# First value stage of an encoder trunk: the norm's vector on GpSimd's queue, the first products reordered, weights piece by piece for both token halves

## The chip, the core and the metric

The kernel runs on one core of a Trainium2 chip. The core has a matrix engine (TensorE, PE in the profile; PEld is its weight load), a vector engine (VectorE, DVE), a scalar engine (ScalarE, ACT), GpSimd (POOL) and SyncE (SP). Each takes its instructions in order from its own queue; SP, ACT and POOL can issue transfers, and all transfers run on the same 16 DMA engines. The metric is the device time of one execution in microseconds (us); lower is better. Times in the profile count from the start of the profiled span.

## The reference, cut to what matters

The input x is one sequence of 256 tokens by 1024 channels in float32. Two layers run, each with two sub-layers, then a last norm. What the change touches is the start of the first sub-layer: a norm and the value columns of one wide projection.

```python
def _rmsnorm(x, g):
    y = x * lax.rsqrt(jnp.mean(x * x, axis=-1, keepdims=True) + EPS)
    return y * g

for layer in range(DEPTH):                       # DEPTH = 2
    h = h + _token_mixer(_rmsnorm(h, norm1[layer]), w_in[layer], ...)
    h = h + _conv_ffn(_rmsnorm(h, norm2[layer]), ...)
return _rmsnorm(h, norm_f)

def _token_mixer(xn, w_in, ...):
    u, q, k, v, g_pool, g_attn = jnp.split(xn @ w_in, SPLITS, axis=-1)
    # pooling mixer on u; sliding-window attention on q, k, v in 3 groups of 4 heads
    # of 128; both branches gated by sigmoids and projected
    return merged @ w_o
```

The columns of v are 1536 wide: three groups of 512, one for each group of heads.

## The kernel before, in words

**Products.** Float32 accuracy is had from a pass format in which an operand is split into a rounded high part and the rest, the low part. A product of two such operands is three matrix multiplications: high by high ("hh"), low x by high weight ("lh"), high x by low weight ("hl"). ACT makes high parts, DVE makes low parts. Almost all of the kernel's work on PE is of this kind, 128 x 128 by 128 x 512.

**Tokens and channels.** The 256 tokens are two halves (t = 0 and 1) of 128, the 1024 channels eight chunks (k = 0 to 7) of 128. A value group is 2 halves x 8 chunks x 3 multiplications = 48 products, which add up in two tiles of PSUM; three groups make 144.

**The first stage** works on x before its norm is known: the gain vector of the norm is multiplied into the weights as they are split (lines 251 to 264), and the tokens' factor 1/rms is applied to the sums when they leave PSUM (`keep_values`, line 945). `begin` (line 367) issues the first transfers: the gain vector (8 rows of 128, tile `grows`) on ACT's queue, then x's first quarter of channels (256 wide) for t = 1 on ACT's queue and for t = 0 on SP's, then alternately first weights (`raw0`, in four chunks) and x (tile `h`), then `raw1` in two parts, `raw2`, `raw3`. PE meanwhile multiplies a constant (line 403, the warm-up), turns the gain vector into a column (line 394; DVE keeps it as `gcol`, line 395), and turns x chunk by chunk (line 787, tile `xt_ps`); ACT casts the turned x to its high part `xuh` (line 793), DVE makes its low part `xul` (line 794).

`begin_values_of_x` (line 767) is an order written out by hand for the first group: `split`, `both`, `turn_x`, `products` and `square` are called one by one, and every engine gets its instructions in that order. `both(k)` makes the high part of weight chunk k on ACT and its low part on DVE; chunk 0's high part is made on DVE (line 261). `square` takes the sum of squares of half a token's channels, on ACT for the first half and on DVE for the second (lines 804 and 808), and GpSimd makes 1/rms (`rs`, tile `rstd`) of them. `whole` adds `xuh` and `xul` to a float32 x (line 822). At the end the four pieces of the second group (two chunks each; `wh` and `wl` 4 to 7) are split.

`first_values` (line 900) turns 1/rms into rows (line 908, `r_ps`), scales x by it and the gain into `x2`, the normed x that the q, k and u projections use (lines 912 to 918), and multiplies groups two and three: for each group all four pieces are fetched, then all products of t = 0, then all of t = 1 (line 930). This function is outside the hand-written order: a scheduler places its instructions. `load_params` (line 409) follows: nine small transfers on SP's queue, and for each layer a turn on PE (line 418) and copies on DVE. `build_bias` (line 424) begins with four transfers and some fifty small copies on GpSimd.

**Weights.** The class `Weights` loads 1 MB at a time into three buffers (`raw`), splits into five pairs of buffers (`wh`, `wl`) and looks three pieces ahead, four where `by_hand` is set. Where `by_hand` is 0 its instructions are also tied behind others (`queue_behind`).

After the third group PE goes on with u, q and k (tile `t_ps`), in a hand-written order again.

Of the kernel before, what the change touches and what calls it, by code (L numbers as in the profile page):

```python
# [10 lines left out]
F32 = mybir.dt.float32  # L11
# [25 lines left out]
WARM = ((P,) * 6, (P // 2,), (P // 2,))  # L37
# [243 lines left out]
def encoder(ctx, tc, x, w_in, w_pool, pool_scale, w_a, w_b, w_o, norm1, norm2, w_up, conv_w,  # L281
# [85 lines left out]
    def begin():  # L367
# [8 lines left out]
        nc.scalar.dma_start(out=rows8, in_=norm1[0].rearrange("(k p) -> k p", p=P))  # L376
# [15 lines left out]
        ps = mmp.tile([P, P], F32, tag="mm", name="gain_ps")  # L392
        warm(ps, ones, WARM[0])
        nc.tensor.transpose(ps[:, 0:KD], rows8, ident[:KD, :KD])
        nc.vector.tensor_copy(gcol, ps[:, 0:KD])
        ps = mmp.tile([P, P], F32, tag="mm", name="warm_ps")
        warm(ps, ones, WARM[1])
        return lambda widths: warm(ps, ones, widths)
# [10 lines left out]
    def load_params():  # L409

        nc.sync.dma_start(out=edge.rearrange("p a b -> p (a b)"), in_=edges[0].partition_broadcast(P))
        for l in range(DEPTH):
# [3 lines left out]
            nc.sync.dma_start(out=rowst[88:96, :], in_=pool_scale[l].rearrange("(f p) -> f p", p=P))  # L416
            pt = mmp.tile([P, 512], F32, tag="mm", name="prm_ps")
            nc.tensor.transpose(pt[:, :96], rowst, ident[:96, :96])
            nc.vector.tensor_copy(prm[:, l, :], pt[:, :96])
            nc.vector.tensor_scalar_mul(hps[:, l, :], prm[:, l, 88:96], 0.5)  # L420

# [345 lines left out]
    def begin_values_of_x():  # L767


        more = begin()  # L770
# [29 lines left out]
        def square(t, n):  # L800
            cc = HALVES[n]
            junk = sm.tile([P, 512], F32, tag="p", bufs=3, name="junk")
            if n == 0:
                nc.scalar.activation(
                    junk, h[:, t, cc], AF.Square, scale=D**-0.5, accum_out=ss[t][:, n : n + 1]
                )
            else:
                nc.vector.scalar_tensor_tensor(
                    out=junk, in0=h[:, t, cc], scalar=1.0 / D, in1=h[:, t, cc],
                    op0=ALU.mult, op1=ALU.mult, accum_out=ss[t][:, n : n + 1],  # L810
                )
# [40 lines left out]

        every = ("hh", "lh", "hl")
        keep = [turn_x((t,), 0, 2) for t in range(2)]
        more(WARM[2])
# [44 lines left out]
    def first_values(rs, raw_x, fs, done, pe, keep_values):  # L900
# [19 lines left out]
        for g in range(NG):  # L920
            held = [W.get() for _ in range(4)] if g + 1 < NG else []
            for t in range(2):
                keep_values(t, g, ps[t], rs)
# [571 lines left out]
```

## Time and profile before

| what | us |
|---|---|
| median of 3 runs | 854.85 (854.73 to 855.8) |
| the profiled execution's own time | 854.77 |
| its span, first to last instruction | 853.0 |
| PE busy in the span | 844.8 |
| DVE, ACT, POOL busy | 620.6, 490.5, 33.6 |
| first product of the first group begins | 5.73 |
| u, q, k products begin | 41.31 |

In rows of the chain in order of time, the columns are start, length, and what ran or was waited for, with a count. In rows of the timeline they are start, length, engine, line, operation, tiles written and read, shapes and count; a bracket tells how long the engine had been idle before it and what ended that. Rows of windows give for a stretch its length, the busy time of PE, PEld, DVE, ACT and POOL with counts, PE's granted clock, the DMA engines' busy share and GB/s. An engine's name with q (SPq, ACTq) is its queue of transfers. PE's matmuls overlap: a product is listed with 0.39 us, but the next starts 0.227 us later.

### The profile page before, as it was taken

The page shows a single profiled execution, that of the slowest core. Times are in us where ns is not written, and L with a number is a line of the kernel's source. Part 1 is how long each engine was busy: PE and PEld are TensorE (multiplying, and loading weights), DVE is VectorE, ACT ScalarE, POOL GpSimd, SP SyncE. Part 2 cuts the span into 40 slices and gives each one's busy share as a digit, 9 for nine tenths or more (in the row PEclk, how much of TensorE's full clock was granted, in tenths as well). Part 3 has the DMA queues.
Part 4 walks back from the last instruction along what each step waited for, and adds up shares of the span by engine and source line. Part 5 has one row for each costly group of instructions (what it writes and reads, how often), then busy time and mean ns, then how long its engine had stood idle before and what let it go on. Part 6 is the DMA issues. An engine that isn't in the chain of part 4 may idle for free.

```text
span 853.0 us, 11006 instructions
## 1 busy us (share of the span) xinstructions
PE 844.8 (99%) x3925; PEld 705.7 (83%) x3925; DVE 620.6 (73%) x885; ACT 490.5 (58%) x723; POOL 33.6 (4%) x96
## 2 busy tenths in 40 slices
PE   9999999999999999999999999999999999999997
PEld 7888888888888888888888888888888888888885
DVE  7958777757765976878655687868567767777774
ACT  7744566654543865657545454577454556556663
POOL 1700000000010000000000000000000100000000
PEclk9999999999999999999999999999999999999999
DMA  9699997895657879986726899868777489799941
GB/s 326 212 302 285 294 292 233 252 293 210 222 209 263 300 250 301 293 284 233 245 100 216 261 280 330 245 226 264 242 257 269 147 289 315 230 288 288 296 145 50
DMA packets 147678, 214.03 MB, mean 251 GB/s; under 512 B 7768, under 2 KB 68640, under 8 KB 147624
## 3 DMA queue, kind: packets, MB, share of 16 engines
q1 hardware_dynamic: 147320, 212.93, 76.8%
q8 instruction: 31, 0.51, 0.2%
q10 hardware_dynamic: 304, 0.40, 0.1%
q14 instruction: 23, 0.19, 0.1%
HBM read 186.02 MB, written 27.28 MB: 250 GB/s over the span
## 4 chain that ended last, share of the span: by engine, by line
PE 98%; DMA 1%; SPq 0%; DVE 0%; ACT 0%; issue 0%; DVEq 0%; ACTq 0%
PE t_ps L691 64%; PE v_ps L691 6%; PE res_ps L610 6%; PE res_ps L608 6%; PE res_ps L609 6%; PE v_ps L930 3%; PE pool_ps L595 1%; PE v_ps L839 1%; PE o_ps L1200 1%; PE s_ps L1152 1%; PE s_ps L1147 1%; PE o_ps L1196 1%; PE xt_ps L522 1%; DMA h<-in_x_dram 1%; PE xt_ps L787 0%; SPq L184 0%
## 5 line engine op out<-in xcount | busy, mean ns | idle before, releaser
L245 DVE TENSOR_TENSOR wl<-raw,wh 128x1024 fp32r<-128x1024 f32 x274 | 332.0, 1221 | 159.0 <-ACT wh L243 158.1
L691 PE MATMUL t_ps<-wh,x 128*128 128x512 f32 x1408 | 438.8, 390 | 0.0
L243 ACT CAST wh<-raw 128x1024 fp32r<-128x1024 f32 x274 | 286.3, 1052 | 211.5 <-PE t_ps L691 146.4
L691 PEld LDWEIGHTS t_ps<-wh,x 128*128 128x128 f32 x1408 | 264.3, 188 | 54.8
L691 PE MATMUL t_ps<-wl,x 128*128 128x512 f32 x704 | 273.9, 389 | 0.0
L691 PEld LDWEIGHTS t_ps<-wl,x 128*128 128x128 f32 x704 | 132.2, 188 | 27.3
L610 PE MATMUL res_ps<-wh,actk 128*128 128x512 f32 (+1 forms) x184 | 70.0, 380 | 0.0
L609 PE MATMUL res_ps<-wl,actq 128*128 128x512 f32 (+1 forms) x184 | 69.9, 380 | 0.0
L608 PE MATMUL res_ps<-wh,actq 128*128 128x512 f32 (+1 forms) x184 | 69.8, 380 | 0.0
L691 PE MATMUL t_ps<-wh,po 128*128 128x512 f32 x128 | 41.4, 395 | 0.0
L608 PEld LDWEIGHTS res_ps<-wh,actq 128*128 128x128 f32 x184 | 34.6, 188 | 6.6
L609 PEld LDWEIGHTS res_ps<-wl,actq 128*128 128x128 f32 x184 | 34.6, 188 | 6.6
L610 PEld LDWEIGHTS res_ps<-wh,actk 128*128 128x128 f32 x184 | 34.6, 188 | 6.6
L487 POOL TENSOR_SCALAR ss<-ss 128x1 f32<-128x1 f32 x8 | 2.2, 279 | 773.5 <-ACT junk L480 773.5
L691 PEld LDWEIGHTS t_ps<-wh,po 128*128 128x128 f32 x128 | 24.0, 188 | 4.9
L1373 ACT ACTIVATE y<-a,prm 128x256 f32<-128x256 f32 x44 | 26.5, 602 | 1.5
L608 PE MATMUL res_ps<-wh,m 128*128 128x512 f32 (+1 forms) x72 | 26.5, 368 | 0.0
L609 PE MATMUL res_ps<-wl,m 128*128 128x512 f32 (+1 forms) x72 | 26.3, 365 | 0.0
L741 DVE STREAM_TRANSPOSE crossing<-t_ps 128x512 f32<-128x512 f32 x40 | 26.2, 693 | 0.0
L610 PE MATMUL res_ps<-wh,m 128*128 128x512 f32 (+1 forms) x72 | 26.0, 366 | 0.0
L691 PE MATMUL v_ps<-wh,x 128*128 128x512 f32 x80 | 25.6, 392 | 0.0
L691 PE MATMUL t_ps<-wl,po 128*128 128x512 f32 x64 | 24.9, 390 | 0.0
(193 smaller groups left out, 931.1 us busy)
## 6 DMA issues: line engine op xcount, KB each, us to landing
raw<-in_w_in_dram SPq DMA_DIRECT2D x58, 1024.0 KB, 6.8
raw<-in_w_up_dram SPq DMA_DIRECT2D x40, 1024.0 KB, 7.1
raw<-in_w_down_dram SPq DMA_DIRECT2D x22, 1024.0 KB, 6.0
crossing<-crossing SPq DMA_DIRECT2D x22, 512.0 KB, 8.5
crossing<-way SPq DMA_DIRECT2D x16, 512.0 KB, 4.8
raw<-in_w_a_dram SPq DMA_DIRECT2D x8, 1024.0 KB, 5.1
raw<-in_w_o_dram SPq DMA_DIRECT2D x8, 1024.0 KB, 7.0
zga<-crossing SPq DMA_DIRECT2D x40, 128.0 KB, 3.7
```

What stands on the lines that cost most here:

```text
L243: inst = nc.scalar.copy(out=h, in_=src)
L245: inst = self.rests[i] = nc.vector.tensor_sub(out=l, in0=src, in1=h.bitcast(F32))
L522: nc.tensor.transpose(pt[:, k, :], xn[:, c0 : c0 + P], ident)
L595: nc.tensor.matmul(out, w(k), x, start=(steps is first and k == 0), stop=(steps is last and k == nk - 1), skip_group_check=turns["rest"],)
L608: nc.tensor.matmul(ps, ah, wh, start=first, stop=False, skip_group_check=on)
L609: nc.tensor.matmul(ps, ah, wl, start=False, stop=False, skip_group_check=on)
L610: nc.tensor.matmul(ps, al, wh, start=False, stop=last, skip_group_check=on)
L691: nc.tensor.matmul(ps, x2[:, 2 * n + j, part, t, :], w[:, j, :], start=(n + m == 0), stop=(n == last and m == 5),)
L741: nc.vector.transpose(out=y[:, t].rearrange("p q c j -> p c q j"), in_=rows[t])
L839: return nc.tensor.matmul(ps[t], a[:, k, t, :], w[:, k % 2, :], start=first, stop=last)
L930: nc.tensor.matmul(ps[t], a[:, k, t, :], w[:, j, :], start=(k + m == 0), stop=(k == KD - 1 and m == 2),)
L1373: nc.scalar.activation(y, a, AF.Identity, bias=b, scale=w1)
```

## The change

**The vector.** Its transfer leaves ACT's queue and is issued from GpSimd's, ahead of the identity that GpSimd builds. The warm-up becomes seven products of 128 columns ahead of the vector's turn and one behind the first turns of x.

**The first group** goes chunk by chunk with both token halves for each kind of product (`one_by_one`). Chunk 1's products come ahead of the second turn of x; high parts of weights are made earlier against the casts of x; all four squares are on ACT and come later; the parameters' transfers are issued within this stage, behind `raw4`.

**The second and third group** are in the hand-written order: a piece is fetched, its 12 products for both halves follow, and between pieces stand a step of the scaling of x, the eviction of the group before, and one layer's parameter turn behind each group.

On ACT, between the second cast of x and the third piece. `m20`, `ybig2` and `at23` are the weights' high parts, two chunks each (the first holds chunks 0 and 1 at first and 2 and 3 next, in two tiles of the same name), `xt_ps` the turned x, `junk` the squares. Before:

```order
L255 ACTIVATE m20_138<-raw0_92,gcol_78 128x512
L793 CAST xuh_123<-xt_ps_149 128x512
L255 ACTIVATE m20_138<-raw0_92,gcol_78 128x512 x2
L804 ACTIVATE junk_170,ss_125<-h_75 128x512
L804 ACTIVATE junk_173,ss_126<-h_75 128x512
L793 CAST xuh_123<-xt_ps_188 128x4x128
L255 ACTIVATE ybig2_205<-raw1_100,gcol_78 128x512
L793 CAST xuh_123<-xt_ps_200 128x4x128
L255 ACTIVATE ybig2_205<-raw1_100,gcol_78 128x512
```

And now:

```order
L255 ACTIVATE m20_138<-raw0_92,gcol_78 128x512 x2
L801 CAST xuh_120<-xt_ps_155 128x512
L255 ACTIVATE m20_138<-raw0_92,gcol_78 128x512
L255 ACTIVATE ybig2_188<-raw1_100,gcol_78 128x512
L801 CAST xuh_120<-xt_ps_176 128x4x128
L801 CAST xuh_120<-xt_ps_183 128x4x128
L255 ACTIVATE ybig2_188<-raw1_100,gcol_78 128x512
L811 ACTIVATE junk_218,ss_122<-h_75 128x512
L811 ACTIVATE junk_221,ss_123<-h_75 128x512
```

Chunk 2's high part now stands ahead of the cast of x chunks 2 and 3, chunk 4's ahead of both casts of the last four chunks, and the squares behind.

On PE, from the first product on (`v_ps` with the lower number is t = 0, the next one t = 1). Before:

```order
L839 MATMUL v_ps_129<-m20_138,xuh_123 128x512
L839 MATMUL v_ps_130<-m20_138,xuh_123 128x512
L839 MATMUL v_ps_129<-m20_138,xul_124 128x512
L839 MATMUL v_ps_130<-m20_138,xul_124 128x512
L787 MATMUL xt_ps_149<-ident_76,h_75 128x128 x4
L839 MATMUL v_ps_129<-m20_138,xuh_123 128x512
```

And now:

```order
L841 MATMUL v_ps_126<-m20_138,xul_121 128x512
L841 MATMUL v_ps_127<-m20_138,xul_121 128x512
L841 MATMUL v_ps_126<-m20_138,xuh_120 128x512
L841 MATMUL v_ps_127<-m20_138,xuh_120 128x512
L841 MATMUL v_ps_126<-m20_138,xul_121 128x512
L841 MATMUL v_ps_127<-m20_138,xul_121 128x512
L795 MATMUL xt_ps_155<-ident_76,h_75 128x128 x4
```

Eight products (the first two are left out above) stand ahead of the turn instead of four.

On POOL, behind the constants, there is one row more, at the top. Now:

```order
L378 DMA grows_88<-in_norm1_dram 8x128
masks.py:197 MEMSET ident_76 128x128
masks.py:199 ISA
masks.py:199 AFFINE_SELECT ident_76<-ident_76 128x128
L815 TENSOR_SCALAR ss_122<-ss_122 128x1
```

The identity that PE's turns read is built behind the transfer's issue.

From the first `t_ps` product on, every engine's order is the same in both kernels.

```diff
-WARM = ((P,) * 6, (P // 2,), (P // 2,))
+WARM = ((P,) * 7, (P,))
@@ begin
-        nc.scalar.dma_start(out=rows8, in_=norm1[0].rearrange("(k p) -> k p", p=P))
         for t, queue in enumerate((nc.sync, nc.scalar)):
             part_of_x(queue, t, slice(0, 256))
+        nc.gpsimd.dma_start(out=rows8, in_=norm1[0].rearrange("(k p) -> k p", p=P))
...
@@ square: all four on ACT
-            if n == 0:
-                nc.scalar.activation(...)
-            else:
-                nc.vector.scalar_tensor_tensor(...)
+            nc.scalar.activation(
+                junk, h[:, t, cc], AF.Square, scale=D**-0.5, accum_out=ss[t][:, n : n + 1]
+            )
@@ begin_values_of_x
+        def one_by_one(*steps):
+            products(*((t, k, (kind,)) for k, kind in steps for t in range(2)))
+
+        gains()
         keep = [turn_x((t,), 0, 2) for t in range(2)]
-        more(WARM[2])
+        more(WARM[1])
...
-        products((0, 0, ("hh",)), (1, 0, ("hh",)), (0, 0, ("lh",)), (1, 0, ("lh",)))
+        one_by_one((0, "hh"), (0, "lh"))
+        both(1)
+        one_by_one((1, "hh"), (1, "lh"))
         keep = turn_x((0, 1), 2, 2)
-        both(1)
+        hi, lo, _ = split(2)
+        hi()
         keep()
-        products((0, 0, ("hl",)), (1, 0, ("hl",)))
-        both(2)
-        products((0, 1, ("hh", "lh")), (1, 1, ("hh", "lh")), (0, 1, ("hl",)), (1, 1, ("hl",)))
+        lo()
+        one_by_one((0, "hl"), (1, "hl"))
         both(3)
+        one_by_one((2, "hh"), (3, "hh"), (2, "lh"))
+        keep = [turn_x((0,), 4, 4)]
+        one_by_one((3, "lh"))
+        keep.append(turn_x((1,), 4, 4))
+        both(4)
+        W.load(5)
+        turn_params = load_params()
+        for k in keep:
+            k()
+        one_by_one((2, "hl"), (3, "hl"))
+        both(5)
+        one_by_one((4, "hh"), (4, "lh"), (4, "hl"))
         square(0, 0)
         square(1, 0)
+        fs = [whole(0, "q0")]
+        both(6)
+        one_by_one((5, "hh"), (5, "lh"), (5, "hl"))
+        both(7)
         square(0, 1)
         pool = square(1, 1)
+        fs.append(whole(1, "k0"))
+        one_by_one((6, "hh"), (6, "lh"), (6, "hl"))
+        products((0, 7, every))
+        products((1, KD - 1, ("hh", "hl", "lh")))
...
@@ first_values (now under manual_schedule with W.by_hand = 1)
+        for g in range(NG - 1):
             ps = [v_tile() for _ in range(2)]
+            for n in range(4):
+                at = 4 * g + n
+                for begun in scales[max(0, at - 1) : at]:
+                    next(begun)
+                i, (wh, wl) = W.get()
+                for begun in scales[max(0, at - 2) : at]:
+                    next(begun)
+                for j in range(2):
+                    k = 2 * n + j
+                    for m, (a, w) in enumerate(((xuh, wh), (xuh, wl), (xul, wh))):
+                        for t in range(2):
                             nc.tensor.matmul(
                                 ps[t], a[:, k, t, :], w[:, j, :], start=(k + m == 0),
                                 stop=(k == KD - 1 and m == 2),
                             )
                 W.free(i)
+                if n == 0:
+                    for t in range(2):
+                        if g == 0:
+                            nc.tensor.transpose(
+                                rows[:, t, :], rs[t][:, 0:1].to_broadcast([P, P]), ident
+                            )
+                    for t in range(2):
+                        keep_values(t, g, done[t], rs)
+            if g < DEPTH:
+                turn_params(g)
+            done = ps
```

More of the change, by code (lines that the diff above doesn't have):

```diff
@@ L905, in first_values, with scale @@
         rows = mmp.tile([P, 2, P], F32, tag="mm", name="r_ps")
[L906 to L909 removed]
+        def scale(k):
             f = fs[k // 4][:, k % 4 : k % 4 + 2]
@@ L978, in encoder @@
         if l == 0:
-            load_params()
             with tc.issue_after(W.behind[1].ins):
```

75 lines of the change are left out of this document (23 added, 52 removed).

## The prediction

> **What bounds the kernel now.** I read the page's shares of the chain first, then the chain in order of time over the first 45 us, because the change touches nothing behind the third value group.
>
> ```profile
> PE 98%; DMA 1%; SPq 0%; DVE 0%; ACT 0%; issue 0%; DVEq 0%; ACTq 0%
> ```
>
> PE carries 98% of the chain, and the change removes no product from it. What can move is the time in which PE has nothing to do, and that lies at the start:
>
> ```profile
> 2.11 5.18 DMA h<-in_x_dram
> 7.29 0.14 issue
> 7.43 0.63 PE xt_ps L787 x4
> 8.05 2.79 PE v_ps L839 x12
> 10.84 0.44 PE xt_ps L787 x4
> 11.28 1.16 PE v_ps L839 x5
> 12.44 0.44 PE xt_ps L787 x4
> 12.88 3.97 PE v_ps L839 x17
> 16.84 0.23 PE v_ps L930
> 17.07 2.27 PE v_ps L839 x10
> 19.33 0.22 PE r_ps L908 x2
> 19.55 11.58 PE v_ps L930 x51
> 31.13 0.17 PE prm_ps L418 x2
> 31.30 10.01 PE v_ps L930 x44
> 41.31 3.85 PE t_ps L691 x17
> ```
>
> From 7.43 on PE never stops. 17.07 to 19.33 gives its pace: 2.27 us for ten products, 0.227 us each. The three groups are 144 products. Four stand ahead of this chain's 7.43; 12 + 5 + 17 + 1 + 10 = 45 more end at 19.33, so the 50th product begins at 19.55, behind the two turns (0.22 us) of the norm vector. From there 51 + 44 = 95 products and 0.17 us of parameter turns lead to 41.31, at full pace. So before has 144 x 0.227 = 32.7 us of products in a stage that ends at 41.31.
>
> Now what comes ahead of 7.43, on PE:
>
> ```profile
> 0.76 2.90 PE L403 MATMUL gain_ps<-const-float32-1.0 128*128 128x128 f32 x12 [0.76 <-PEq L1477]
> 3.59 0.22 PE L394 MATMUL gain_ps<-ident,grows 8*128 8x8 f32 x1
> 5.21 0.44 PE L787 MATMUL xt_ps<-ident,h 128*128 128x128 f32 x2 [0.81 <-DMA h<-in_x_dram]
> 5.73 0.89 PE L839 MATMUL v_ps<-m,xuh 128*128 128x512 f32 x2
> ```
>
> The reader is to see two waits, both for x: the second token half's first quarter (0.81 us), and the second quarter of both halves (the chain's DMA until 7.29).
>
> **The most there is to gain.** The first product cannot move: it waits for the first weight chunk, which lands at 5.10 (DVE row below) in both kernels, since the change puts no transfer of SP's queue ahead of it. It begins at 5.7. With no later wait at all the stage would take 32.7 + 12 late turns of x (0.44 for four in the rows at 10.84 and 12.44, so 1.32) + 0.22 + 0.17 = 34.4 us and end at 40.1: 1.2 us, 0.14%, less than the 0.2% (1.7 us) that a measurement of this kernel tells from no change.
>
> **Part by part: the start.** ACT's queue loses the vector's issue, so x's second half is issued 0.62 us earlier:
>
> ```profile
> 0.72 0.59 ACTq L376 DMA_DIRECT2D grows<-in_norm_dram  x1
> 1.34 0.37 ACTq L374 DMA_DIRECT2D h<-in_x_dram  x1
> 6.13 0.72 ACT L255 ACTIVATE m<-raw,gcol 128x512 fp32r<-128x512 f32 x1
> 8.09 0.59 ACT L793 CAST xuh<-xt_ps 128x512 fp32r<-128x512 f32 x1 [1.24 <-PE xt_ps L787]
> 8.57 1.34 ACT L255 ACTIVATE m<-raw,gcol 128x512 fp32r<-128x512 f32 x2
> 9.81 0.62 ACT L804 ACTIVATE junk<-h 128x512 f32<-128x512 f32 x1
> 11.31 0.59 ACT L793 CAST xuh<-xt_ps 128x512 fp32r<-128x512 f32 x1 [0.18 <-PE xt_ps L787]
> 11.80 0.72 ACT L255 ACTIVATE ybig<-raw,gcol 128x512 fp32r<-128x512 f32 x1
> ```
>
> That takes away the 0.81 us wait at 5.21, but the second product then still follows the first at 5.93 instead of 6.12: 0.2 us. More is won by putting chunk 1's products ahead of the turn that waits for x: its high part is made at 6.13 + 0.72 = 6.85, four products from 5.7 end at 6.6, so PE waits 0.25, and about eight products instead of four are done near 7.8, where before waited until 7.43. At this point the new order is 0.5 us ahead. The seventh 128-wide warm-up and the removed two 64-wide ones lie ahead of 5.10 and cost nothing: 12 records in 2.90 us, so 0.48 us for one, and the warm-up ends near 4.1.
>
> **The vector on GpSimd's queue.** No row shows a transfer issued there. Lower bound: ACT's was issued at 0.72 and PE used it at 3.59, right behind the warm-up, so it had landed within 2.87 us. Upper bound: the x piece on ACT's queue took from 1.34 to PE's use at 5.21, 3.87 us; with an issue as long as ACT's (0.59) that makes 0.72 + 0.59 + 3.87 = 5.2. I take 4.3, the middle, as the vector is small like the first but its queue unseen. The identity is made behind this issue on the same engine and is wanted at 4.1, so it is hidden. If the vector lands at g, then by the rows at 3.59, 3.85, 5.10 and 5.73 the first product starts at g + 0.26 + 0.24 + 0.05 + 0.60 = g + 1.15; up to g = 4.5 that is hidden behind the weight's 5.10. The Trainium skill, "DMA: Bandwidth & Descriptors", section "Anatomy of one DMA — SWDGE (gpsimd) path", puts such a transfer at a fixed 2.0 us plus its bytes; by that (an estimate) it lands at 2.7, the sum stays as it is, and the chance I give below to a late vector would halve.
>
> **Chunks 2 to 4, where it is given back.** ACT now runs chunk 2's high part ahead of the cast of x that chunk 2's products need (order above), where before it cast at 8.09 first. Chunk 2's weights were used at 8.57 behind that cast, so they land at 8.57 or earlier; x was there at 7.29. I take 8.1: high part until 8.8, cast until 9.4, PE's next product at 9.4 while its work ends near 9.1: a wait of 0.3, and 0.2 more for chunk 3's high part. The 0.5 us won are gone. Then chunk 4's high part, the first of the second load, stands ahead of both casts of the last four x chunks. Call its landing L. DVE and ACT durations for what follows:
>
> ```profile
> 3.85 0.17 DVE L395 COPY gcol<-gain_ps 128x8 f32<-128x8 f32 x1 [3.00 <-PE gain_ps L394]
> 5.10 0.48 DVE L261 TENSOR_SCALAR m<-raw,gcol 128x512 fp32r<-128x512 f32 x1 [1.08 <-DMA raw<-in_w_in_dram]
> 12.55 0.75 DVE L256 SCALAR_TENSOR_TENSOR ybig<-raw,gcol,ybig 128x512 fp32r<-128x512 f32 x1
> 13.53 0.69 DVE L794 TENSOR_TENSOR xul<-xt_ps,xuh 128x512 fp32r<-128x512 f32 x1 [0.23 <-ACT xuh L793]
> 14.15 0.75 DVE L256 SCALAR_TENSOR_TENSOR ybig<-raw,gcol,ybig 128x512 fp32r<-128x512 f32 x1
> 14.82 1.22 DVE L822 TENSOR_TENSOR xu<-xuh,xul 128x1024 f32<-128x1024 f32 x1
> 15.96 1.41 DVE L256 SCALAR_TENSOR_TENSOR at<-raw,gcol,at 128x512 fp32r<-128x512 f32 x2
> ```
>
> High part L + 0.05 to L + 0.77; on DVE its low part starts at L + 0.82 and holds DVE 0.67 (14.15 to 14.82), then two low parts of x at 0.62 (13.53 to 14.15) and 0.69: they end at L + 0.82 + 0.67 + 0.62 + 0.69 = L + 2.80, and PE's 28th product, which multiplies the second of them, starts at L + 2.85. L is at most 11.75 (the row at 11.80 followed a cast with no wait). From below, the bytes queued up to it are 2.62 MB:
>
> ```profile
> 2.00:10.40 8.40, 7.24 (x36) 5.62 (x36) 4.43 (x9) 4.80 (x9) 0.00 (x0) 1.00 0.97 307
> ```
>
> 307 GB/s over 8.4 us is 2.58 MB, with 0.04 before, so L is not before 10.4. The x transfer that landed at 7.29 was the end of 1.05 MB, which this rate moves by about 5.5 to 6.0: landing trails by 1.3 us or more there. 10.4 + 1.1 gives L = 11.5, near the upper end. So the 28th product starts at 14.35 and, if nothing stops PE, the 50th at 14.35 + 22 x 0.227 = 19.34. Before began it at 19.55, with 0.22 us of turns done that the new order still owes: 19.33 against 19.34. The sum is zero.
>
> **Second and third group.** The squares of the second half go from DVE to ACT (0.62 each, the row at 9.81), behind chunk 7. ACT reaches piece 4 some 2.4 us later than before's 15.25 (four squares at 0.62), near 17.7; PE wants it at 19.1. DVE starts chunk 5's low part at L + 2.11 + 0.62 = 14.23; with it (0.67), a sum for the whole x (14.82 to 15.96, 1.14), two low parts (1.34) and the second sum (1.14) it reaches piece 4's first low part at 18.52 and ends it at 19.27. PE wants it with the 51st product, at 19.56: hidden by 0.3 us only. From there each piece serves both halves: 12 x 0.227 = 2.72 us of PE for 2 x 0.67 us of DVE, where the first half of before's second group used a piece in 1.36 us. The scaling of x (the same instructions) is spread between the pieces, and DVE's backlog before the third stage, which was hidden, stays hidden. The parameter turns stand at the ends of groups two and three, near 30 and 41 us. Their nine small transfers and one of the bias table move ahead of raw5, whose issue slips behind the last of them. The first row is that last one's issue in the timeline, the second is from the list of the weight loads of the first 24 us:
>
> ```profile
> 20.62 0.27 SPq L416 DMA_DIRECT2D prow<-in_pool_scale_dram  x1
> ```
>
> ```profile
> DMA to landing us min/median/max: 4.4/6.3/9.1
> ```
>
> So raw5 is issued near 20.9. Even with the slowest load's 9.1 us it lands at 30, and its pieces are wanted at 19.34 + 70 x 0.227 = 35.2 or later. Same turns on PE: zero. Everything behind the third group is issued in the same order as before and only shifts.
>
> **Sum.** 0.0 us against the profiled execution's own 854.77 (span 853.0 and 1.8 around it), which stands 0.08 under the median of 854.85. I predict 854.85.
>
> **Rivals.** (1) The gain stays: L earlier than 11.1 and chunk 2 landed by 7.4, so that neither cast is late; then PE ends the stage between 40.1 and 40.9, 853.7 to 854.4. For it: the x pieces may flow better when both queues start at once. Against: 97% DMA share in the row above. (2) The vector comes late. Beyond g = 5.4 the early part is no longer covered (first product g + 1.15, plus 27 products and 1.32 of turns, plus 0.4 of waits, is g + 9.0 against 14.35) and each microsecond costs one; g = 7.1 makes 1.7 us, 856.6, and decides for slower. For it: GpSimd has issued nothing in this trace, and its queue's first use is unseen. Against: both bounds end under 5.4. Its price could double by PE's pace: the warm-up's 0.24 us a record against 0.11 for the same width at 10.84 says that PE starts slow. The Trainium skill, "TensorE: Matmul & The Clock Gate", Part 1, has PE fall to half its clock after about 3.4 us idle; that would be met only for g past 7.5 and would add up to 1.7 us (an estimate); the granted clock in these rows reads 1.00 throughout and can't confirm it. (3) Piece 4 or a parameter turn stalls PE: DVE's 0.3 us of cover is used up, +0.2 to +1 us, 855.1 to 855.9.
>
> **Chances.** Forecast, within 0.4 us: 0.58. Rival 1, a gain of 0.4 to 1.2: 0.20. Rival 2: 0.16, of it 0.10 beyond 1.7 us. Rival 3: 0.04, half of it beyond when several stalls add up. A gain over 0.2%, which needs the first weights earlier than anything here explains: 0.02. So faster 0.02, same 0.58 + 0.20 + 0.06 + 0.02 = 0.86, slower 0.12. Range 853.7 (best gain) to 856.6 (vector at 7.1); the likeliest alone is 854.4 to 855.3.
>
> **What would show it.** Right: first product at 5.7, eight products before the turn near 7.8, a wait of PE near 9.2 for the cast and one near 14 for x's low part, r turns near 22, first t_ps at 41.2 to 41.5. Wrong: the gain transpose waiting for a DMA past 5 us; or no wait of PE between 8 and 15, with the first t_ps near 40.5; or PE waiting on DVE at 19 to 20 us.

## The result: 0.15% slower, and the profile after

Forecast was no change. Measured: median 856.54 us over 21 runs (855.51 to 857.1) against 855.05 us over 21 runs of the kernel before (854.38 to 856.3); the ratio is 1.0015, with a 95% interval of 1.0009 to 1.0022. That is a small loss, but the interval leaves no change out.

The profiled execution took 856.37 us, with a span of 854.3. Against the profiled 854.77 and 853.0 of before, the 1.60 us fall into three parts: the u, q, k products start at 42.35 and not at 41.31 (1.04); from there to the end of the span it is 811.95 and not 811.69 us (0.26); and 2.07 us and not 1.77 lie outside the span (0.30). Two thirds are where the prediction looked, in the first stage. First the chain in order of time of the changed kernel (start, length, what ran or was waited for, count):

```profile
4.87 7.39 DMA raw<-in_w_in_dram
12.29 0.73 ACT ybig L255
13.05 0.75 DVE ybig L256
13.80 1.21 DVE xul L802 x2
15.05 5.06 PE v_ps L841 x21
20.11 2.72 PE v_ps L944 x12
22.83 0.22 PE r_ps L952 x2
23.05 8.18 PE v_ps L944 x36
...
42.27 0.09 PE prm_ps L424
42.35 17.76 PE t_ps L699 x78
```

Until 12.27 the chain is the transfer of chunk 4's weights; then come its high part on ACT, its low part on DVE, two low parts of x, and PE's 28th product at 15.05. Before had x's landing at 7.29 in that place and nothing but PE behind it. Then the rows of the timeline that answer to the prediction's steps, in the same kernel:

```profile
1.25 0.76 POOL L378 DMA_DIRECT2D grows<-in_norm_dram  x1 [0.81 <-POOLq L1504]
...
4.72 0.19 PE L397 MATMUL gain_ps<-ident,grows 8*128 8x8 f32 x1 [0.73 <-DMA grows<-in_norm_dram]
4.84 0.66 PE L795 MATMUL xt_ps<-ident,h 128*128 128x128 f32 x4
...
5.79 0.73 PE L841 MATMUL v_ps<-m,xuh 128*128 128x512 f32 x2
...
7.79 0.60 PE L795 MATMUL xt_ps<-ident,h 128*128 128x128 f32 x4
8.15 2.46 PE L841 MATMUL v_ps<-m,xuh 128*128 128x512 f32 x8
10.45 0.62 PE L841 MATMUL v_ps<-m,xul 128*128 128x512 f32 x2
...
12.29 0.72 ACT L255 ACTIVATE ybig<-raw,gcol 128x512 fp32r<-128x512 f32 x1 [2.47 <-DMA raw<-in_w_in_dram]
```

PE waits 0.73 us for the vector, the first product still starts at 5.79, the second turn of x begins at 7.79 behind eight products, the eight products from 8.15 take until 10.45, and ACT waits 2.47 us for chunk 4.

### The profile page after: what moved, and what is told of

The parts are those of the page before. It is cut to its first block, busy times and chain, and to the rows that moved or that the text cites. A ratio compares the mean times of both kernels' runs of the same rounds, so it can differ in the third digit from the quotient of the medians.

```text
span 854.3 us, 11008 instructions
## 1 busy us (share of the span) xinstructions
PE 846.0 (99%) x3925; PEld 705.9 (83%) x3925; DVE 619.3 (72%) x881; ACT 491.3 (58%) x727; POOL 34.9 (4%) x97
## 4 chain that ended last, share of the span: by engine, by line
PE 97%; DMA 1%; SPq 0%; DVE 0%; ACT 0%; issue 0%; DVEq 0%; ACTq 0%
PE t_ps L699 64%; PE v_ps L699 6%; PE res_ps L618 6%; PE res_ps L617 6%; PE res_ps L616 6%; PE v_ps L944 3%; PE pool_ps L603 1%; DMA raw<-in_w_in_dram 1%; PE o_ps L1227 1%; PE s_ps L1179 1%; PE s_ps L1174 1%; PE o_ps L1223 1%; PE xt_ps L530 1%; PE v_ps L841 1%; SPq L374 0%; SPq L184 0%
```

## The experiments

Seven theories came up in the course of it. A: the order on ACT costs, since chunk 4's high part stands ahead of the casts. B: the changed queues delay the weights. C: PE's pace at the start; it runs either at full pace (0.227 us a product) or at about half of it, and the moment of the step differs between executions. D, its rival: something lands late. E: the bias table's small pieces delay the weights. F: GpSimd's queue delays them. G: x's second token half does, because it starts 0.62 us earlier.

The table has one row for each kernel. "Turns" is the length of the row of the first four turns of x, or of two (x2), a measure of PE's pace (0.66 or less for four at full pace, 0.44 or less for two); "chunk 4" the start of its high part on ACT, with w where ACT had waited for the weights, so that they had just landed.

| kernel | vector's turn | first product | turns | chunk 4 | first t_ps | median, us | ratio to before |
|---|---|---|---|---|---|---|---|
| before | 3.59 | 5.73 | 0.44 (x2) | 11.80 | 41.31 | | |
| changed | 4.72 | 5.79 | 0.66 | 12.29 w | 42.35 | 856.54 | 1.0015 (1.0009 to 1.0022) |
| e11 changed, again | 4.95 | 6.31 | 1.11 | 12.30 w | 42.66 | 856.63 | 1.0012 (1.0003 to 1.0020) |
| e1 vector on ACT | 4.02 | 5.68 | waits inside | 11.87 w | 41.94 | 855.34 | 1.0002 (0.9993 to 1.0010) |
| e17 the same, again | 4.02 | 5.45 | 0.44 (x2) | 11.50 w | 41.54 | 855.24 | 0.9997 (0.9988 to 1.0006) |
| e2 before, vector on GpSimd | 4.87 | 6.66 | 1.06 | 12.77 | 42.31 | 856.11 | 1.0011 (1.0002 to 1.0020) |
| e5 before, new groups 2, 3 | 3.59 | 5.68 | waits inside | 12.81 | 42.58 | 855.76 | 0.9998 (0.9989 to 1.0007) |
| e6 new start, old groups 2, 3 | 4.91 | 6.28 | 1.11 | 12.21 w | 44.26 | 858.06 | 1.0029 (1.0017 to 1.0040) |
| e3 changed, casts first | 4.62 | 5.69 | 0.66 | 12.72 | 41.48 | 857.12 | 1.0014 (1.0006 to 1.0023) |
| e4 e3 and vector on ACT | 4.00 | 5.70 | 0.44 (x2) | 12.78 | 41.54 | 855.15 | 1.0000 (0.9991 to 1.0009) |
| e7 e3, ten warm-ups | 5.30 | 6.65 | 1.11 | 13.78 | 42.54 | 856.36 | 1.0011 (1.0002 to 1.0020) |
| e8 e2, ten warm-ups | 5.03 | 6.30 | 0.61 | 11.90 | 41.33 | 855.23 | 0.9994 (0.9985 to 1.0003) |
| e10 before, nine warm-ups | 4.36 | 5.63 | 0.65 | 11.83 | 41.37 | 854.85 | 0.9993 (0.9984 to 1.0002) |
| e13 e5, nine warm-ups | 4.69 | 5.97 | 0.60 | 11.78 w | 41.26 | 855.21 | 1.0000 (0.9991 to 1.0008) |
| e9 changed, bias later | 4.64 | 6.01 | 1.11 | 11.61 w | 42.62 | 856.42 | 1.0013 (1.0004 to 1.0022) |
| e14 changed, nine warm-ups | 4.77 | 5.87 | 0.66 | 12.67 w | 42.75 | 856.25 | 1.0010 (1.0002 to 1.0019) |
| e15 e14, bias later | 4.88 | 6.18 | 0.86 | 12.52 w | 42.63 | 856.42 | 1.0013 (1.0004 to 1.0022) |
| e16 e1, spare copy on GpSimd | 4.02 | 5.93 | 0.69 (x2) | 11.58 | 42.87 | 855.59 | 1.0000 (0.9991 to 1.0009) |
| e18 e14, x's half later | 5.35 | 6.41 | 0.66 | 11.24 w | 41.54 | 855.38 | 1.0006 (0.9997 to 1.0015) |
| e12 three places mended | 4.87 | 6.01 | 0.66 | 12.30 | 42.08 | 855.63 | 1.0004 (0.9995 to 1.0013) |

The marks come from one profiled execution each, medians and ratios from all runs of the kernel beside runs of before on the same chip. The profiled execution isn't always a typical one: it was the fastest of its kernel's runs in e3 and e18, the slowest in e7 and e14. Before's median in those comparisons was 855.39 to 855.76.

### Which part: the vector's queue, or the groups

e1 undoes the vector's move:

```diff
+        nc.scalar.dma_start(out=rows8, ...)
         for t, queue in enumerate((nc.sync, nc.scalar)):
             part_of_x(queue, t, slice(0, 256))
-        nc.gpsimd.dma_start(out=rows8, ...)
```

> The changed kernel with one thing undone: the norm vector is loaded on ACT's queue ahead of x's second half, as before. Theory A (the order on ACT costs: chunk 4's high part waits there for weights ahead of the casts, and the landing L is late whatever queue carries the vector): L stays near 12.3, PE's 28th product near 15.05, the first t_ps near 42.3, 856.4 us. Theory B (the queues delay the weights: two queues that start at once and GpSimd's one push L from at most 11.75 to 12.27): L returns to 11.75 or less, the 28th product to 14.5, the first t_ps to 41.8 or less, 855.9 us or less.

Measured: 855.34, no longer told from before, chunk 4 at 11.87, first t_ps 41.94: nearer to theory B's numbers (11.75 and 41.8 or less) than to A's. The loss goes with the vector's queue. e2 is the other side: the kernel before with this one line moved.

```diff
-        nc.scalar.dma_start(out=rows8, ...)
         for t, queue in enumerate((nc.sync, nc.scalar)):
             part_of_x(queue, t, slice(0, 256))
+        nc.gpsimd.dma_start(out=rows8, ...)
```

> The kernel before with one thing changed: the norm vector on GpSimd's queue, behind the issues of x's first quarters. Theory A: the first product stays near 5.75 and the weights of chunk 4 are still there when ACT comes to them, so 854.9 to 855.1 us, no change. Theory B: chunk 4's high part starts later than 11.80 with a wait for a DMA (up to 12.3), the products of chunk 4 come 0.3 to 0.5 us later, 855.3 to 855.6 us.

Measured: 856.11, slower (1.0002 to 1.0020), more than either theory gave. The first product came at 6.66 and not at 5.75. The timeline and the chain of this kernel:

```profile
4.87 0.24 PE L394 MATMUL gain_ps<-ident,grows 8*128 8x8 f32 x1 [1.21 <-DMA grows<-in_norm_dram]
...
5.52 1.06 PE L787 MATMUL xt_ps<-ident,h 128*128 128x128 f32 x4
```

```profile
6.90 1.70 PE v_ps L839 x4
8.60 0.44 PE xt_ps L787 x4
...
42.31 17.91 PE t_ps L691 x79
```

PE waits 1.21 us for the vector and then works at half pace: four products in 1.70 us (0.42 each, not 0.227), and the turns of x need 1.06 us first and 0.44 behind 8.60. That was new, and gave theory C.

e5 takes the second part of the change alone: `first_values` as after, and in before's first group

```diff
         W.load(5)
+        turn_params = load_params()
```

> The kernel before with the second part of the change alone: second and third value group piece by piece for both token halves, x scaled in between, the parameter loads ahead of the sixth weight load, the norm vector's turns behind the first piece. First group, vector and squares as before. Theory A (nothing of the loss lies in these groups): no wait of PE between 19 and 41 us, the first t_ps within 0.1 us of 41.3, the same time as before within 0.3 us. Rival (the groups cost): the first t_ps at 41.6 or later, 0.3 to 1 us slower.

Measured: 855.76, before's median in that comparison (855.76). Rows of its chain:

```profile
5.92 1.81 PE v_ps L845 x4
7.73 0.85 PE xt_ps L793 x4
...
23.07 0.22 PE r_ps L950 x2
...
42.58 17.53 PE t_ps L697 x77
```

The first t_ps misses the expected 41.3, since PE was at half pace until past 8.5 us (four products in 1.81 us, four turns in 0.85); this execution took 856.09. From the r turns to the first t_ps it needed 19.51 us, the changed kernel 19.52 (22.83 to 42.35): no wait. So no cost of the groups shows here. Before's own times in that comparison were read anew: 854.4 to 855.0 in one cluster, 855.5 to 856.5 in another, perhaps as PE was at full pace early or late; e10 below asks that.

e6 is the new start with before's `first_values` and `load_params`:

```diff
-                W.by_hand = 1
                 x2 = first_values(*begun, keep_values)
-                W.by_hand = 0
...
         if l == 0:
+            load_params()
```

> The changed kernel's start and first group (vector on GpSimd's queue, chunk 4 ahead of the casts, all squares on ACT) with the kernel before's second and third group and parameter loads. Theory A: the whole loss is here; chunk 4's high part starts near 12.2, the first t_ps near 42.2, 856.3 to 856.6 us. Rival (the groups cost): the time falls back to at most 855.7.

Both theories missed: 858.06, slower than the whole change. Its chain shows why:

```profile
18.25 1.26 POOL ss L811
...
20.91 0.95 POOL rstd L812
...
21.91 0.32 PE r_ps L910
...
44.26 15.95 PE t_ps L693 x70
```

With all squares on ACT, GpSimd ends 1/rms at 21.86, and PE, whose r turns stand ahead of the second group in before's order, waits for it. In the changed kernel they stand behind the first piece, at 22.83, and nothing waits. The two parts need each other; a time for the start alone can't be had this way.

### The order on ACT

e3 puts the casts of the last x chunks ahead of chunk 4, e4 moves the vector back as well:

```diff
+        for k in keep:
+            k()
         both(4)
         W.load(5)
         turn_params = load_params()
-        for k in keep:
-            k()
```

> The changed kernel with the two casts of the last four x chunks put ahead of chunk 4's high part on ACT (and with them their low parts ahead of chunk 4's low part on DVE). Theory A: the casts run from about 11.1 to 12.3 while ACT waits for nothing, the 25th product starts right behind the high part at L + 0.77 = 13.05, the 28th at 13.75 and not 15.05, the first t_ps comes 1.0 to 1.3 us earlier, near 41.2, and 855.2 to 855.5 us against 856.5. If the groups two and three or anything behind them carried the loss, the time would stay at 856.4.

> Both: the casts ahead of chunk 4's high part, and the vector on ACT's queue. Theory A: as with the casts alone, 855.2 to 855.5 us. Theory B adds its part: L at 11.75 or less, the 28th product near 13.3, the first t_ps near 40.7, 854.7 to 855.0 us, under the kernel before.

In e3's trace the mechanism came as theory A said: chunk 4's products from 13.49, first t_ps 41.48, 0.87 us ahead of the changed kernel, and 855.5 us in that execution. But only four of eleven runs were like it (855.5 to 855.94); seven took 857.08 to 857.83. e4 gave 855.15, ten of eleven within 854.98 to 855.50. Theory A is right for the execution in the trace and doesn't carry the median; the vector's queue does.

### PE's pace

e7 (on e3, first pair of lines) and e8 (on e2, second pair) lengthen the warm-up to ten products so that PE has work until the vector lands; e10 has nine in the kernel before:

```diff
-WARM = ((P,) * 7, (P,))
+WARM = ((P,) * 10, (P,))
...
-WARM = ((P,) * 6, (P // 2,), (P // 2,))
+WARM = ((P,) * 10, (P // 2,), (P // 2,))
```

> The kernel with the casts ahead of chunk 4's high part (vector on GpSimd's queue), and ten instead of seven 128-wide warm-up products, so that PE has work until the vector lands near 4.6. In the run without them the times lay in two clusters, 855.5 to 855.9 and 857.1 to 857.8. Theory C (while PE waits for the late vector it falls to its slow pace, 0.42 instead of 0.227 us a product, in most executions, and eight products at it cost 1.6 us): the upper cluster goes, median 855.3 to 855.7. Theory D (the upper cluster is a late landing of the vector itself or of the weights): both clusters stay, median near 857.

> The kernel before with the vector on GpSimd's queue and ten instead of six 128-wide warm-up products. Without them PE waited 1.21 us for the vector and then ran four turns in 1.06 and four products in 1.70 us. Theory C: with PE kept busy the turns take 0.66 us or less and the products 0.23 each, the first product starts near 6.0, PE waits for x until 7.3 as in the kernel before, first t_ps near 41.3, 854.9 to 855.3 us. Theory D: the products stay slow or x and weights are late, first t_ps at 42 or later, 855.8 or more.

> The kernel before with nine instead of six 128-wide warm-up products. Its own times so far lie in two clusters, 854.2 to 855.0 and 855.5 to 856.5. Theory C (the clusters are the time at which PE changes from its slow to its full pace, and work without a gap ahead of x makes it change early): the upper cluster goes, all runs within 854.3 to 855.3, median 854.5 to 854.9, under the kernel before by 0.5 to 1 us. Rival (the clusters come from transfers or from later stages): both stay, median as before.

e8: 855.23, all runs within 854.93 to 855.72, where e2 had none under 855.85. Its timeline, and from its chain the products and the end of the stage:

```profile
5.45 0.61 PE L787 MATMUL xt_ps<-ident,h 128*128 128x128 f32 x4
```

```profile
6.30 1.29 PE v_ps L839 x4
...
41.33 18.81 PE t_ps L691 x83
```

The turns take 0.61 and not 1.06, the stage ends at before's 41.3. The vector lands late as in e2, so it was the pace that cost. e10: all eleven runs within 854.55 to 855.32, median 854.85, where before had 854.17 to 857.09 beside it: the upper cluster is gone, as theory C said and its rival did not. e7: the upper cluster is gone too (nothing over 856.54, where e3 had seven at 857.08 or more), but the median is 856.36, not 855.3 to 855.7: in its trace the twenty warm-up records all ran at half pace, ended at 5.37 and pushed the first product to 6.65. Of theory C the mechanism held, not the price.

e11 ran the changed kernel once more:

> The changed kernel once more, unchanged, as the measure for the runs beside it: 856.2 to 856.8 us, chunk 4's high part at 12.0 to 12.4, the first t_ps at 42.1 to 42.6. If PE is slow at the start in this execution (turns of x at 1.0 us for four, not 0.66), the 28th product still starts between 15.0 and 15.5, since it waits for chunk 4.

```profile
4.95 0.24 PE L397 MATMUL gain_ps<-ident,grows 8*128 8x8 f32 x1 [0.86 <-DMA grows<-in_norm_dram]
5.12 1.11 PE L795 MATMUL xt_ps<-ident,h 128*128 128x128 f32 x4
...
6.31 1.20 PE L841 MATMUL v_ps<-m,xuh 128*128 128x512 f32 x2
...
12.30 0.72 ACT L255 ACTIVATE ybig<-raw,gcol 128x512 fp32r<-128x512 f32 x1 [0.90 <-DMA raw<-in_w_in_dram]
```

```profile
1.24 3.57 DMA grows<-in_norm_dram
...
6.66 3.06 PE v_ps L841 x8
...
13.98 6.43 PE v_ps L841 x28
...
42.66 17.53 PE t_ps L699 x77
```

Same kernel, another execution, nearly the same time (856.64), and another chain. The timeline and the chain show the wait for the vector, then half pace: eight products in 3.06 us from 6.66, where full pace needs 1.82. From 13.98 PE never waits, though chunk 4 was again late (12.28): the 28th product, the eighth from there, comes near 15.5, later than chunk 4 would allow (12.28 + 2.78). So the changed kernel has two losses side by side, each enough for most of the delay.

The Trainium skill ("TensorE: Matmul & The Clock Gate", Part 1) has PE start at half its clock and reach the full one after a busy window of about 3.4 us that runs freely, so that the moment differs from run to run. The traces agree with the half pace (0.42 to 0.227) and with the spread: full pace was there by the turns at 4.84 of the changed kernel, only near 8.60 in e2 and past 9 in e11. A wait of PE is not what decides it: behind its wait of 0.73 us the changed kernel has full pace, while e5, with no wait listed on PE from its warm-up to 10 us, has half pace until past 9. The granted clock reads 1.00 in all these stretches and shows none of it.

### Chunk 4's weights

e9 moves the bias table's transfer, e14 lengthens the changed kernel's warm-up to nine, e15 does both:

```diff
         W.load(5)
+        W.fifth = W.sent
...
-            with tc.issue_after(W.behind[1].ins):
+            with tc.issue_after(W.behind[1].ins), tc.issue_after(W.fifth.ins):
                 bias = build_bias()
```

> The changed kernel with one thing moved: the first small transfer of the bias table (128 pieces of four bytes), which stands on SP's queue ahead of the fifth weight load and is issued at 8.27 us, goes behind the sixth. Vector on GpSimd's queue as in the change. Theory E (these small pieces delay chunk 4's weights): they land at 11.9 or earlier, PE's 28th product starts at 14.7 or earlier, 0.3 to 0.4 us under the changed kernel. Theory F (GpSimd's queue delays them): landing 12.2 to 12.3 and the changed kernel's time.

> The changed kernel with nine instead of seven 128-wide warm-up products, and nothing else. Theory C (the late vector leaves PE idle, and PE then stays at its slow pace until after 9 us in most executions): PE has its full pace by the time of the first product, which starts at 5.8 to 6.2; the loss that stays is chunk 4's late landing, so the 28th product still starts near 15.0: 855.8 to 856.4 us, 0.2 to 0.7 under the changed kernel. If the pace had no part in it: 856.6 us as before.

> The changed kernel with nine warm-up products and with the bias table's small transfer behind the sixth weight load: both suspected causes taken away, while the vector stays on GpSimd's queue and the order of the products is the change's. Theory C with theory E: chunk 4's weights at 11.6 to 11.9, the 28th product at 14.4 to 14.7, the first t_ps at 41.7 to 42.0, 855.2 to 855.6 us, a full microsecond under the changed kernel. If something else carries the loss, it stays at 856.3 or more.

e9: the weights landed at 11.59, as theory E said, but the time stayed (856.42), with PE at half pace in the trace. e14 took the pace away: first product 5.87 and turns at 0.66, and 856.25, 0.3 us under the changed kernel, with intervals that overlap; in the trace its weights were the latest of all (12.65) and its 28th product came at 15.43. e15 should have had neither, and still had 12.50 and 856.42. Theory E falls: with the bias transfer out of the way the weights were early in one trace and late in the other.

What goes with the late weights is a dip of the DMA engines' share. In the following rows of the windows view (stretch, length, busy time of PE, PEld, DVE, ACT and POOL with counts, clock, DMA share, GB/s) the stretch is 6 to 8 us; first the changed kernel, then e14, then e17:

```profile
6.00:8.00 2.00, 2.00 (x10) 1.58 (x10) 1.80 (x4) 0.59 (x1) 0.00 (x0) 1.00 0.80 273
```

```profile
6.00:8.00 2.00, 2.00 (x10) 1.50 (x11) 1.88 (x4) 0.83 (x3) 0.00 (x0) 1.00 0.83 265
```

```profile
6.00:8.00 2.00, 1.75 (x7) 1.13 (x8) 1.74 (x3) 0.72 (x1) 0.00 (x0) 1.00 1.04 345
```

0.80 and 0.83 with the vector on GpSimd's queue alone, 1.04 with it on ACT's. The five traces in which the weights landed at 12.19 or later have 0.80 to 0.90 there; e9, with early weights, has 0.94; all traces with the vector or a copy ahead of x on ACT's queue have 0.96 to 1.06. e16 adds an unused copy of the vector on GpSimd's queue to e1, e17 is e1 again beside it, and e18 leaves the vector on GpSimd's queue in e14 and puts an unused copy on ACT's queue, so that x's piece behind it is issued at 1.35 again (the line on nc.scalar is e18's, that on nc.gpsimd e16's):

```diff
+        spare = sm.tile([KD, P], F32, tag="spare", bufs=1, name="spare")
+        nc.scalar.dma_start(out=spare, ...)
         for t, queue in enumerate((nc.sync, nc.scalar)):
             part_of_x(queue, t, slice(0, 256))
+        nc.gpsimd.dma_start(out=spare, ...)
```

> The changed kernel with the vector on ACT's queue, and beside it a second, unused copy of the vector loaded on GpSimd's queue, for which nobody waits. Theory F (a transfer through GpSimd's queue slows the others: in the runs that have it the DMA engines were busy 0.75 to 0.97 of the time from 6 to 8 us, in those without it 0.93 to 1.04): the share falls below 0.92 between 6 and 8 us, chunk 4's weights land at 12.2 to 12.6, 0.4 us or more over the run beside it without the copy: 855.8 to 856.2 us. Otherwise (the late weights come with the early start of x, or by chance): landing at 11.7 to 11.9 and the time of the run without the copy.

> The changed kernel with the vector on ACT's queue once more, as the measure for the run with the unused copy: 855.1 to 855.6 us, chunk 4's weights at 11.7 to 11.9, the DMA share at 0.95 or more from 6 to 8 us.

> The changed kernel with nine warm-up products, and on ACT's queue an unused copy of the vector ahead of x's second token half, so that this piece of x is issued at 1.34 us again and not at 0.72. The vector that is used stays on GpSimd's queue. Theory G (the weights are late because this piece of x starts 0.62 us earlier and takes its share of the DMA engines from SP's queue): chunk 4's weights land at 11.5 to 11.9, the 28th product at 14.3 to 14.7, 855.2 to 855.6 us against 856.25 with nine warm-up products alone. Otherwise: weights at 12.2 to 12.7, 856.1 to 856.6 us.

e16: weights there by 11.58, share 1.00; theory F falls as a cause by itself. (Its median is 0.35 us over e17's. The one trace, of an execution of 856.49, has half pace until past 9 us; whether that makes the median is not shown.) e18:

```profile
6.00:8.00 2.00, 1.94 (x11) 1.44 (x10) 1.92 (x5) 1.95 (x4) 0.00 (x0) 1.00 1.06 363
```

```profile
0.72 0.59 ACTq L377 DMA_DIRECT2D spare<-in_norm_dram  x1
1.35 0.37 ACTq L374 DMA_DIRECT2D h<-in_x_dram  x1
...
11.24 0.73 ACT L255 ACTIVATE ybig<-raw,gcol 128x512 fp32r<-128x512 f32 x1 [0.99 <-DMA raw<-in_w_in_dram]
```

Share 1.06, weights at 11.22, first t_ps 41.54, median 855.38 against before's 855.44 beside it. The timeline shows what the edit does, 0.6 us on ACT's queue ahead of x. Theory G holds in this pair: with x's second half issued at 0.72 the weights behind it on the other queue come later. It is one trace on each side, e14's of its slowest run and e18's of its fastest. And the mean rate doesn't explain all of it: from 0 to 12 us e14 moved 266 GB/s and e18 280, which at the 402 GB/s from 10 to 12 us is 0.4 us of transfer (an estimate), and the landings are 1.43 us apart. Three of e18's eleven runs took 856.59 to 856.88; none of these has a trace, and whether they were runs at half pace is open (the vector came late, at 5.21, in the one that has).

### Attempts at a version that gains

e12 mends three places (vector on ACT's queue, nine warm-ups, and, in the diff, chunk 4's high part between the two casts), e13 is before with the new groups and nine warm-ups:

```diff
-        both(4)
+        keep[0]()
+        hi, lo, _ = split(4)
+        hi()
+        keep[1]()
+        lo()
...
-        for k in keep:
-            k()
```

> The change with its three weak places mended: vector on ACT's queue, nine warm-up products, and chunk 4's high part between the two casts of the last x chunks on ACT. Theory C and E: first product near 5.8, chunk 4's weights at 11.9 or earlier, no wait of PE over 0.2 us between 8 and 20 us, first t_ps at 41.0 to 41.4, 854.5 to 854.9 us: under the kernel before, and equal to it with nine warm-up products (854.85).

> The kernel before with the second part of the change (groups two and three piece by piece, parameter loads early) and nine instead of six warm-up products, so that PE's pace at the start is the same in all executions. With the groups free of cost: 854.85 us as without them (median 854.85 with nine warm-up products alone), first t_ps at 41.3 to 41.4. If they cost: 855.2 or more.

e12 missed: 855.63, t_ps 42.08. Its warm-up ran at half pace to 4.94, so the vector that was there in time was turned at 4.87 and the first product came at 6.01. But e18, with its first product at 6.41, has its first t_ps 0.54 us earlier, so that isn't what held e12 up. Its chain runs through the edit itself:

```profile
13.54 0.69 DVE xul L802
14.23 0.67 DVE ybig L256
...
14.94 4.83 PE v_ps L841 x20
```

Chunk 4's low part now stands on DVE behind both low parts of x, and PE's 29th product, which reads it, can't start before 14.94. e13's trace is that of before to 0.05 us (t_ps 41.26, span 853.0); its median of 855.21 stands 0.36 over e10's from another comparison, with intervals that overlap, so a cost of the groups up to that size can't be ruled out, and none is seen in a trace. No kernel beats before beyond its interval; the nearest is e10, before with three more warm-up products, at 0.9993 (0.9984 to 1.0002).

## Why the prediction was wrong, step by step

**Most there is to gain, the start.** Right in the profiled execution: first product 5.79 (5.7 given), the turn behind eight products at 7.79 (7.8), the vector landed near 4.6 (4.3 taken, 3.6 to 5.2 given; 4.72 less the 0.14 us between landing and turn in e11's rows) and was covered. What was to be given back at chunks 2 and 3, 0.5 us, was: eight products from 8.15 to 10.45 are 0.48 over full pace. (The 0.2% that the text takes for the least that can be told from no change was too much: the measured 0.15% has an interval of 1.0009 to 1.0022.)

**The step that failed in that execution: the landing L.** L was taken as 11.5 with an upper end of 11.75, because before's row at 11.80 had no wait. It was 12.27. What followed was as worked out: L + 2.85 to the 28th product was given, 15.05 - 12.27 = 2.78 measured. So 0.77 us are the term L. The upper end was carried over from before as if the change did nothing to these weights; but it starts x's second half earlier on the other queue, by the very 0.62 us that the text booked as won for x, and the late landings go with that (five of six traces; how, is open). Rival 1 even hoped that transfers would flow better when both queues start at once. They flowed worse (e14 against e18, 12.65 against 11.22).

**Behind the 28th product** the chain has 21 products in 5.06 us, and full pace is 21 x 0.227 = 4.77. Only a part of these 0.29 us is a stop of PE. The chain lets a piece begin where the record before it ends, and a product's record is 0.39 us long while the next product starts after 0.227; so behind a wait the chain's times run 0.16 us after the starts. The timeline has the starts; first the changed kernel, then before:

```profile
19.95 0.61 PE L944 MATMUL v_ps<-wh,xuh 128*128 128x512 f32 x2
...
42.14 0.48 PE L699 MATMUL t_ps<-wh,x 128*128 128x512 f32 x1
```

```profile
19.17 0.38 PE L908 MATMUL r_ps<-ident,rstd 128*128 128x128 f32 x2
...
41.15 0.39 PE L691 MATMUL t_ps<-wh,x 128*128 128x512 f32 x1
```

The 49th product starts at 19.95, 4.90 behind the 28th, so PE stopped for 0.13 us where the sum had it never stop. The other 0.16 us are a slip of the sum itself: it set a start (14.35 + 22 x 0.227 = 19.34) against a time of before's chain (19.33), where the timeline has 19.17. Counted in starts, the forecast of zero was a loss of 0.16. The first t_ps is late by 42.14 - 41.15 = 0.99 us: 0.70 up to the 28th product (15.05 for 14.35, the 0.77 of L less 0.07), 0.13 and 0.16.

**The second step that failed: what a late vector costs.** The text let a vector be free up to 4.5 and cost 1 us for each microsecond past 5.4, at full pace; it set the half pace aside as something met only by an idle of 3.4 us, with a vector at 7.5. The traces show half pace behind gaps of 0.55 to 1.21 us (e9, e11, e2), far under 3.4: in these executions PE had not reached full pace yet. Behind gaps of 0.49 to 0.73 in e18, e3 and the changed kernel it had. In e11 the vector landed at 4.81, for which the text has a cost of nothing, and the first t_ps was 1.35 us late. So rival 2 was right in its place (the vector) and its sign, with the wrong price. The warning was in the text, in the sentence on the warm-up's 0.24 us a record, but as a doubling of a cost that was thought to be hidden.

**Groups two and three**, rival 3: right, nothing. The r turns at 22.83 had no wait. That they had to move because of the squares (e6) was not seen.

**What was not in the sum at all**: 0.3 us outside the span. In all runs of the changed kernel 2.07 to 2.20 us lie outside it, in all of before 1.73 to 1.84, and 1.75 to 1.83 in e18. The other kernels with the vector on GpSimd's queue, no copy on ACT's and the new groups (e3, e7, e9, e14, e15) have 2.07 to 2.19; e2 and e8, the kernel before with the vector moved, 1.73 to 1.85; all others at most 1.96. So the vector's move costs this only together with the rest of the change. Its cause stays open, as does that of the 0.26 us between the first t_ps and the end of the span. And before's own time was taken as one number, where it is two clusters 1.2 us apart.

**Which of the two losses the median has.** Each alone holds the stage back: e14's trace has late weights at full pace (first t_ps 42.75), e9's early weights at half pace (42.62). So taking away one (e14: 0.3 us) uncovers the other; with the vector back on ACT's queue (e1, e17), or a copy there and the longer warm-up (e18), the loss is no longer measurable. These three also win back the 0.3 us outside the span. How often each of the two sets the time of a run is not shown, since each kernel has one trace or two.

## What to carry to other kernels

A transfer that is moved off a queue lets the next one on that queue start earlier, and here weights on another queue then landed later: look at who lands later, not only at who starts sooner. At the very start PE can run at half pace for its first ten products, and no column of the clock shows it: read the pace from the rows, and try a longer warm-up, which took the slow executions away in e8 and e10, though not the half pace in e7's trace. Where two causes each suffice for a delay, undoing one of them measures little: take both away, then put them back one by one. And don't set a start of the timeline against a time of the chain.

## What the runs showed of the hardware

- PE's pace at the start has two values (0.42 and 0.227 us for a 128x512 product), and the step came anywhere from before 4.43 us (e10, whose 18 warm-up records took 3.67 us where e12's took 4.18) to past 9 (e5, e11, e16); the granted clock read 1.00 throughout.
- A 4 KB transfer on GpSimd's queue kept POOL 0.76 us for its issue at 1.24 and landed 3.25 to 3.98 us from the start of that issue; on ACT's queue the vector was there within 2.87 us of its issue.
- Chunk 4's weights, issued at the same place of SP's queue, landed between 11.22 and 12.65 us. With x's second half issued at 0.72 on the other queue they came at 12.19 or later in five traces (changed, e6, e11, e14, e15) and at 11.59 in one (e9; e8, where it was 11.88 or earlier, has before's order); with it at 1.34 never later than 11.85 where the landing shows. What in the DMA engines makes it so is open.
